# An RWKV-7, convolution and mLSTM block on one core: modulation rows as TensorE products spread through the recurrent chains, a later projection moved into the last chain, and the first dense products by halves

## The chip, the cores and the metric

The kernel runs on one core of one Trainium2 chip. Its five engines have queues of their own: TensorE (PE, with its weight loads PEld), VectorE (DVE), ScalarE (ACT), GpSimd (POOL) and SyncE (SP), which issues the DMAs. An engine takes its instructions in the order of the program and waits on semaphores for the others. The metric is the device time of one execution in microseconds (us).

## The reference

One block is computed in fp32 for 512 tokens of width 1024, with 256 context tokens that only feed the two recurrences. Six modulation vectors come from `silu(c) @ w_ada + b_ada`: shift and scale ahead of the mixers, a gate on their sum, shift and scale ahead of the MLP, and a gate on it.

```python
mod_x = jnp.split((jax.nn.silu(c) @ w_ada[l] + b_ada[l])[:, None, :], N_MOD, axis=-1)
mod_c = jnp.split(jax.nn.silu(c_ctx) @ w_ada[l] + b_ada[l], N_MOD, axis=-1)
h = _rmsnorm(x, g_norm1[l]) * (1.0 + mod_x[1]) + mod_x[0]
hc = _rmsnorm(ctx, g_norm1[l]) * (1.0 + mod_c[1]) + mod_c[0]
u_rw, u_cv, u_ml, u_gate = jnp.split(h @ w_in[l], [OFF_CV, OFF_ML, OFF_GATE], axis=-1)
...
yb = _conv_branch(u_cv, cv_dw[l], cv_db[l], cv_lnw[l], cv_lnb[l], rows)   # silu(layernorm(conv31(a * sigmoid(g))))
x = x + mod_x[2] * _merge(u_gate, ya, yb, yc, p_a[l], p_b[l], p_c[l], w_out[l])
h = _rmsnorm(x, g_norm2[l]) * (1.0 + mod_x[4]) + mod_x[3]
x = x + mod_x[5] * _mlp(h, w_mlp1[l], w_mlp2[l])
```

`ya` is the RWKV-7 mixer (8 heads of 64, a recurrence over the tokens in both directions), `yc` the mLSTM mixer (chunks of 64), and `_merge` is `(sigmoid(ga) * ya@pa + sigmoid(gb) * yb@pb + sigmoid(gc) * yc@pc) @ w_out`.

## The kernel before

Activations lie transposed: a tile holds 128 features by 512 tokens. A dense product is split into high and low parts of both operands: `whalf` (L147) loads half a weight block (`raw`, 128 x 512), ACT makes its high part `whi` (L152) and POOL the low part `wlo` (L153), and PE adds `hi*hh`, `hi*hl` and `lo*hh` for each of eight k-tiles, 24 products of 128 x 512 for a block of 128 columns.

The stages, in program order:
- **Front** (L164 to L231). `norm` scales the rows of x and transposes them on PE (`pl`, L202). For each quarter q of the first two modulation vectors eight products `pr` (L215) with a stationary operand of two columns (c and c_ctx) make a row of 512; four small transposes `pm` (L220) turn it into columns, and `modulate` makes `hh` and `hl` for two k-tiles. All four quarters, then the context norm, stand ahead of the first dense product (L262).
- **Convolution gates and taps** (L273 to L300): two dense blocks make a gated tile `z` (L281), for i = 0 and 1, and 62 DVE operations the depthwise taps; the other two tiles follow in the mLSTM stage, with their taps, from stored `z`. The four results go to DRAM as `yb`.
- **RWKV features**, then **mLSTM** with its dense blocks. `rw.ctx(0)` and `rw.lat(0)` make the first RWKV pair's gram products `pg` (L973) and invert small triangular matrices on DVE.
- **Four chains** (`weave`, L1142). Chain j walks the 12 chunks of head pair j in both directions. A step is a batch of small fp32 products `ch` (L1100, L1106, L1115), with an ACT or DVE operation between batches. Each chain has 36 rounds. Between the batches `weave` puts steps of the next pair's gram and inversion (`PACE` per round), of the tail of the pair before (its group norm), and a number of dense products from one generator: `DENSE[j]` per chain, evenly over the rounds, and `EXTRA[j]` after them. That generator yields the gate products `dg` (L512), then the projections `dp` of the convolution and mLSTM outputs (L591). `paced` keeps a woven instruction behind the batch that it follows.
- **Chain 3** also weaves `conv_norm` (L533, the layer norm and silu of the convolution) and `modulations` (L611): DVE sums `sc[k] * wad` (L608) over 128 x 512 tiles of `w_ada`, eight for each of six quarters, a product with ones closing each. The remaining `dp`, the tail of chain 3 and the remaining sums follow as a drain.
- **Merge and MLP** (`merge`, L1229): the RWKV output's projection `pd` (L682), `w_out` (`pt`, L1268), the second norm, MLP1 (`pd`, L1337), in which the last two quarters of modulation sums (`last_modulation`) stand with one product `pmr` (L644) each, and MLP2 (`pt`).

In PSUM, direction 0 of the gram writes pool PS (tag g), direction 1 pool PSC (tag g).

## Time and profile before

| | |
|---|---|
| time, median of 3 runs | 1372.29 us (1367.92 to 1378.71) |
| the profiled execution | 1377.12 us, its span 1375.3 us |
| PE busy | 1252.9 us (91%) |
| PE weight loads | 969.6 us (71%) |
| DVE busy | 849.2 us (62%) |
| ACT, POOL busy | 511.8 us (37%), 585.7 us (43%) |
| DMA | 187.85 MB, mean 137 GB/s |

Busy shares are means over the span. A row of the chain of waits names what the last work to end was released by, followed back in time. The clock is the TensorE clock that was granted, as a share of the full one; a stretch's mean between 0.5 and 1 is a mixture of two levels. Two PE records belong to one fp32 product.

### The profile page before, as it was taken

The page shows a single profiled execution, that of the slowest core. Times are in us where ns is not written, and L with a number is a line of the kernel's source. Part 1 is how long each engine was busy: PE and PEld are TensorE (multiplying, and loading weights), DVE is VectorE, ACT ScalarE, POOL GpSimd, SP SyncE. Part 2 cuts the span into 40 slices and gives each one's busy share as a digit, 9 for nine tenths or more (in the row PEclk, how much of TensorE's full clock was granted, in tenths as well). Part 3 has the DMA queues.
Part 4 walks back from the last instruction along what each step waited for, and adds up shares of the span by engine and source line. Part 5 has one row for each costly group of instructions (what it writes and reads, how often), then busy time and mean ns, then how long its engine had stood idle before and what let it go on. Part 6 is the DMA issues. An engine that isn't in the chain of part 4 may idle for free.

```text
span 1375.3 us, 21700 instructions
## 1 busy us (share of the span) xinstructions
PE 1252.9 (91%) x8004; PEld 969.6 (71%) x8004; DVE 849.2 (62%) x1509; ACT 511.8 (37%) x1048; POOL 585.7 (43%) x547
## 2 busy tenths in 40 slices
PE   6999989786999886999899988889999999999997
PEld 1587877565888775667566665667888878888886
DVE  2599588889266993797977857678366534300202
ACT  4434556632222231243342444422354444322322
POOL 0443334426755441332433435533456544444442
PEclk9999999898999997999998998999999999999999
DMA  9221588732633314323431244787434433433422
GB/s 375 65 69 58 134 270 255 246 104 62 186 99 97 111 64 120 110 93 101 143 110 49 85 145 136 259 263 249 131 112 156 142 100 95 153 104 96 131 95 89
DMA packets 101457, 187.85 MB, mean 137 GB/s; under 512 B 10708, under 2 KB 29396, under 8 KB 100328
## 3 DMA queue, kind: packets, MB, share of 16 engines
q1 hardware_dynamic: 101352, 186.47, 42.9%
q8 instruction: 63, 1.03, 0.3%
q14 instruction: 42, 0.34, 0.1%
HBM read 148.64 MB, written 29.40 MB: 129 GB/s over the span
## 4 chain that ended last, share of the span: by engine, by line
PE 45%; DVE 14%; DMA 5%; issue 3%; ACT 1%; POOL 1%; SPq 0%; DVEq 0%; POOLq 0%; ACTq 0%
PE pt L1268 16%; PE pd L1337 13%; PE dg L512 5%; DMA wad<-wada 4%; DVE N L1019 3%; DVE tmp L1017 2%; PE pg L973 2%; PE ch L1100 1%; PE pd L682 1%; DVE N L1012 1%; PE ch L1106 1%; DVE accm L608 1%; PE dl L262 1%; PE pbk L998 1%; PE ch L1115 1%
## 5 line engine op out<-in xcount | busy, mean ns | idle before, releaser
L153 POOL TENSOR_TENSOR wlo<-raw,whi 128x512 fp32r<-128x512 f32 x296 | 435.5, 1477 | 555.5 <-ACT whi L152 488.9
L152 ACT CAST whi<-raw 128x512 fp32r<-128x512 f32 x296 | 182.0, 618 | 318.7 <-PE pt L1268 118.8
L262 PE MATMUL dl<-hh,wlo 128*128 128x512 f32 (+1 forms) x368 | 149.7, 407 | 10.8 <-POOL wlo L153 10.8
L262 PE MATMUL dl<-hh,whi 128*128 128x512 f32 (+1 forms) x368 | 151.4, 412 | 2.7 <-ACT kT L758 1.9
L262 PE MATMUL dl<-hl,whi 128*128 128x512 f32 (+1 forms) x368 | 148.5, 403 | 0.0
L1337 PE MATMUL pd<-h2l,whi 128*128 128x512 f32 (+1 forms) x272 | 103.3, 381 | 0.7 <-POOL h2l L1320 0.7
L1337 PE MATMUL pd<-h2h,wlo 128*128 128x512 f32 (+1 forms) x272 | 102.7, 379 | 0.0
L1337 PE MATMUL pd<-h2h,whi 128*128 128x512 f32 (+1 forms) x272 | 101.5, 380 | 0.2 <-ACT h2h L1317 0.2
L1363 DVE TENSOR_TENSOR x<-pt,modb 128x512 f32<-128x512 f32 x8 | 5.5, 690 | 154.7 <-PE pt L1268 154.7
L1268 PE MATMUL pt<-whi,h1h 128*128 128x512 f32 x256 | 99.6, 389 | 0.0
L1268 PE MATMUL pt<-whi,h1l 128*128 128x512 f32 x256 | 99.6, 389 | 0.0
L1268 PE MATMUL pt<-wlo,h1h 128*128 128x512 f32 x256 | 99.1, 389 | 0.0
L262 PEld LDWEIGHTS dl<-hh,wlo 128*128 128x128 f32 (+1 forms) x368 | 70.7, 192 | 26.0 <-POOL wlo L153 11.2
L262 PEld LDWEIGHTS dl<-hh,whi 128*128 128x128 f32 (+1 forms) x368 | 71.2, 193 | 18.6 <-ACT kT L758 2.1
L262 PEld LDWEIGHTS dl<-hl,whi 128*128 128x128 f32 (+1 forms) x368 | 70.8, 192 | 15.2 <-issue 1.5
L608 DVE SCALAR_TENSOR_TENSOR accm<-wad,sc,accm 128x512 f32<-128x512 f32 x56 | 59.1, 1056 | 35.2 <-DMA wad<-wada 34.6
L1113 POOL TENSOR_TENSOR sps<-SV,PL 64x128 f32<-64x128 f32 x88 | 40.0, 454 | 85.1 <-DVE SV L1116 81.9
L1341 DVE TENSOR_TENSOR relu<-relu 128x512 f32<-128x512 f32 x32 | 38.9, 1218 | 55.8 <-ACT relu L1340 55.7
L512 PE MATMUL dg<-hl,whi 128*128 128x512 f32 x144 | 66.5, 462 | 0.0
L512 PE MATMUL dg<-hh,whi 128*128 128x512 f32 x144 | 65.7, 456 | 0.0
L512 PE MATMUL dg<-hh,wlo 128*128 128x512 f32 x144 | 65.6, 456 | 0.0
L1019 DVE TENSOR_TENSOR N<-N,tmp 128x30 f32<-128x30 f32 (+14 forms) x120 | 58.1, 484 | 3.0
(389 smaller groups left out, 2792.3 us busy)
## 6 DMA issues: line engine op xcount, KB each, us to landing
raw<-wblk SPq DMA_DIRECT2D x296, 256.0 KB, 2.9
wad<-wada SPq DMA_DIRECT2D x64, 256.0 KB, 4.0
wada<-wada SPq DMA_DIRECT2D x8, 1024.0 KB, 13.4
BK<-kb SPq DMA_DIRECT2D x16, 384.0 KB, 5.2
sp_bk<-BK SPq DMA_DIRECT2D x8, 768.0 KB, 5.2
BK<-sp_bk SPq DMA_DIRECT2D x8, 768.0 KB, 4.1
sp_g<-gt SPq DMA_DIRECT2D x24, 256.0 KB, 2.0
sp_al<-al SPq DMA_DIRECT2D x8, 640.0 KB, 4.6
```

Of the source, the lines that this page charges most:

```text
L152: A.copy(hi[:, :], raw[:, :])
L153: G.tensor_tensor(lo[:, :], raw[:, :], hi[:, :], ALU.subtract)
L262: PE.matmul(ps_[0:M, :], lhsT=w[:, ko:ko + M], rhs=x[seg][:, k, :], start=(n == 0), stop=(n == 3 * KT - 1))
L512: yield lambda w=w, x=x, k=k, ko=ko, n=n: PE.matmul(ps[:, :], lhsT=w[:, ko:ko + P], rhs=x[:, k, :], start=(n == 0), stop=(n == 3 * KT - 1))
L608: V.scalar_tensor_tensor(o, t[:, :], sc[:, k, 0:1], o, ALU.mult, ALU.add)
L973: PE.matmul(ps[hf, i, :, :], lhsT=BK[dd, c, x, :], rhs=al[:, c] if lat else AL[d][dd, 8 + c:9 + c, :], start=True, stop=True)
L1017: V.tensor_tensor(tv, N[:, s + 1:32, s:s + 1].to_broadcast([P, n, s]), N[:, s:s + 1, 0:s].to_broadcast([P, n, s]), ALU.mult)
L1019: V.tensor_tensor(N[:, s + 1:32, 0:s], N[:, s + 1:32, 0:s], tv, ALU.add)
L1113: last["Pool"] = G.tensor_tensor(sps[hf], SV[d][hf, c, :, :], PL[hf, c, :].unsqueeze(2).to_broadcast([64, 2, CH]), ALU.mult)
L1268: PE.matmul(pss[i][:, :], lhsT=x[:, k, ts_], rhs=w[:, :], start=(k == 0 and n == 0), stop=(k == nk - 1 and n == 2))
L1337: PE.matmul(ps[:, ts_], lhsT=w[:, ko:ko + P], rhs=x[:, k, ts_], start=(k == 0 and n == 0), stop=(k == 7 and n == 2))
L1341: V.tensor_tensor(t[:, :], t[:, :], t[:, :], ALU.mult)
```

## The change

- **Front.** A product of the modulation now has a stationary operand of 32 columns (`scz`, c and c_ctx followed by columns of the next k and zeros) and writes the PSUM rows from 32 * (k mod 4): four consecutive products use four groups of columns of the array. A product with `sel` adds the four partial rows and turns them. All eight `wada` tiles have buffers; the context rows are loaded behind the fifth of them, three weight halves behind the sixth. The first three dense blocks (two gates and one value) are computed by halves: k-tiles 0 to 3 behind quarter 1, k-tiles 4 to 7 behind quarter 3. The context norm stands ahead of quarter 2.
- **Convolution norm.** `conv_norm` moves from chain 3 to behind the second pair of taps; its result goes to DRAM as `yb`. Its tiles share space with the first RWKV pair's.
- **Modulations.** The 64 DVE sums (48 in chain 3 and its drain, 16 in MLP1) become 64 products on PE, one yielded after six gate products, loaded into two `wad` buffers (the load of block n + 2 is issued behind block n). Their rows are closed with `sel`; two vectors go through DRAM and are broadcast on loading. MLP1 has none left.
- **Chains.** `DENSE` becomes 120, 120, 120, 270, so that nearly all `dp` stand in chain 3; `ld` has three buffers. Direction 1 of the gram writes the bank with tag m of pool PS.

PE in the front: the modulation products of the last quarters (`pr`), the closing ones (`pm`), the transposes of context rows (`pl` from `ct`) and the first dense products (`dl`). Before:

```order
L202 MATMUL pl<-cst,xt_180 128x128
L215 MATMUL pr<-wada,sc 2x512 x8
L220 MATMUL pm<-cst,row 128x2 x4
...
L202 MATMUL pl<-cst,xt_180 128x128
L220 MATMUL pm<-cst,row 128x2 x4
L202 MATMUL pl<-cst,ct_198 128x128
L202 MATMUL pl<-cst,ct_200 128x128
L202 MATMUL pl<-cst,ct_198 128x128
...
L202 MATMUL pl<-cst,ct_198 128x128
L202 MATMUL pl<-cst,ct_200 128x128
L262 MATMUL dl<-hh_164,whi 128x512
L262 MATMUL dl<-hl_166,whi 128x512
```
After:

```order
L234 MATMUL pl<-cst,xt_189 128x128
L174 MATMUL pr<-wada,scz 32x512 x8
L189 MATMUL dl<-hh_170,whi 128x512
L189 MATMUL dl<-hl_172,whi 128x512
L189 MATMUL dl<-hh_170,whi 128x512
L189 MATMUL dl<-hl_172,whi 128x512
L234 MATMUL pl<-cst,ct_201 128x128 x2
L254 MATMUL pm<-sel,row 128x2 x4
L189 MATMUL dl<-hh_170,wlo 128x512
...
L189 MATMUL dl<-hh_170,wlo 128x512
L234 MATMUL pl<-cst,ct_203 128x128 x2
L174 MATMUL pr<-wada,scz 32x512 x8
L189 MATMUL dl<-hh_170,whi 128x512
```
All 32 `pr` and the 16 context transposes stood ahead of the first `dl`; now the first `dl` stand behind the third quarter's `pr` and among the transposes, and the fourth quarter's eight `pr` follow 36 of them.

PE in the first steps of chain 0: batches of the chain (`ch`), gate products (`dg`) and, after, one modulation product (`pq`). Before:

```order
L1100 MATMUL ch_4813<-SV_4797,AL_3240 64x64
L1100 MATMUL ch_4813<-SV_4797,AL_3243 64x64
L1100 MATMUL ch_4814<-SV_4798,AL_3241 64x64
L1100 MATMUL ch_4814<-SV_4798,AL_3244 64x64
L512 MATMUL dg<-hh_164,whi 128x512
L512 MATMUL dg<-hl_166,whi 128x512
L1106 MATMUL ch_4813<-xc_4845,LT_3238 64x64 x2
L1106 MATMUL ch_4814<-xc_4849,LT_3238 64x64 x2
L512 MATMUL dg<-hh_164,wlo 128x512
L512 MATMUL dg<-hh_164,whi 128x512
L512 MATMUL dg<-hl_166,whi 128x512
```
After:

```order
L1135 MATMUL ch_4893<-UV_4874,BKt_3329 64x64
L1135 MATMUL ch_4893<-UV_4874,BKt_3330 64x64
L1135 MATMUL ch_4894<-UV_4875,BKt_3329 64x64
L1135 MATMUL ch_4894<-UV_4875,BKt_3330 64x64
L174 MATMUL pq<-wad,scz 32x512
L623 MATMUL dg<-hh_170,whi 128x512
L623 MATMUL dg<-hl_172,whi 128x512
L623 MATMUL dg<-hh_170,wlo 128x512
L1120 MATMUL ch_5007<-SV_4877,AL_3320 64x64
L1120 MATMUL ch_5007<-SV_4877,AL_3323 64x64
```
A round has three gate products in both; the modulation product is one more, beside a batch or between gate products.

PE at the end of chain 3: the outputs of the chain (`py`), its tail (`pm`, `pv`, `pm`), projections of the two other mixers (`dp`) and of RWKV (`pd`). Before (the tail with its neighbours):

```order
L591 MATMUL dp<-yh,whi 128x512
L1193 MATMUL pm<-y,cst 128x512
L591 MATMUL dp<-yl,whi 128x512
...
L591 MATMUL dp<-yh,whi 128x512
L1201 MATMUL pv<-cst,ysq 128x2 x4
L591 MATMUL dp<-yl,whi 128x512
...
L591 MATMUL dp<-yh,wlo 128x512
L1210 MATMUL pm<-cst,rb 128x128 x4
L591 MATMUL dp<-yh,whi 128x512
```
After (the last of `dp`, then the tail):

```order
L663 MATMUL dp<-yh,whi 128x512
L663 MATMUL dp<-yl,whi 128x512
L663 MATMUL dp<-yh,wlo 128x512
...
L1101 MATMUL py<-AL_4870,SV_4878 64x64
L1102 MATMUL py<-LR_4871,UU 64x64
L1210 MATMUL pm<-y,cst 128x512
L1218 MATMUL pv<-cst,ysq 128x2 x4
L1227 MATMUL pm<-cst,rb 128x128 x4
L703 MATMUL pd<-yh,whi 128x512
```
The tail's products stood 22 to 39 `dp` products apart; now they follow one another and the 18 last `dp`, and `pd` stands behind them. Counted over PE's order: gate products in chains 0 to 3 before 110, 104, 120, 98, after 114, 101, 135, 82; modulation products 16, 19, 21, 8; `dp` in chain 3 31 before and 174 after, behind it 161 and 18.

The diff, cut:

```diff
+    def partial(ps, k, w):
+
+
+        g = slice(32 * (k % 4), 32 * (k % 4) + 32)
+        PE.matmul(ps[g, :], lhsT=scz[:, 2 * k:2 * k + 32], rhs=w, start=(k < 4), stop=(k >= 4))
...
+    def first_products(half, wts, pss=None):
+
+        pss = pss or [PSD.tile([P, NT], F32, tag="d", name="dl", bufs=ND) for _ in FIRST]
+        for ps, (hi, lo) in zip(pss, wts):
+            for k in range(4):
+                ko, kt = k * P, half * 4 + k
+                for n, (w, x) in enumerate(((hi, hh), (hi, hl), (lo, hh))):
+                    PE.matmul(ps[:, :], lhsT=w[:, ko:ko + P], rhs=x[0][:, kt, :],
+                              start=(kt == 0 and n == 0), stop=(kt == KT - 1 and n == 2))
...
-        t = S0.tile([P, 4, 512], F32, tag="wada", name="wada", bufs=6)
+        t = S0.tile([P, 4, 512], F32, tag="wada", name="wada", bufs=8)
         SY.dma_start(t[:, :, :], wada[q].rearrange("p (k m) -> p k m", k=4))
         wa.append(t)
-    for i in range(2):
-        t = S0.tile([P, D], F32, name=f"ct{i}")
-        SY.dma_start(t[:, :], cin[i])
-        xt.append(t)
+        if q == 4:
+            for i in range(2):
+                t = S0.tile([P, D], F32, name=f"ct{i}")
+                SY.dma_start(t[:, :], cin[i])
+                xt.append(t)
+        if q == 5:
+            first = [whalf(b, 0) for b in FIRST]
...
         for k in range(KT):
-            PE.matmul(pr[:, :], lhsT=sc[:, k, :], rhs=wa[q * 2 + k // 4][:, k % 4, :], start=(k == 0), stop=(k == KT - 1))
-        row = S0.tile([2, NT], F32, tag="row", name="row", bufs=2)
+            partial(pr, k, wa[q * 2 + k // 4][:, k % 4, :])
+        row = S0.tile([P, NT], F32, tag="row", name="row", bufs=2)
         A.copy(row[:, :], pr[:, :])
...
         for i in range(4):
-            PE.transpose(pt[:, i, :], row[:, i * P:(i + 1) * P], ident[0:2, 0:2])
+            PE.matmul(pt[:, i, :], lhsT=row[:, i * P:(i + 1) * P], rhs=sel[:, :], start=True, stop=True)
         ks = slice(2 * q, 2 * q + 2)
         V.tensor_tensor(modc[:, ks, :], pt[:, 0:2, :], C("b_ada", 2 * q, 2).unsqueeze(2).to_broadcast([P, 2, 2]), ALU.add)
...
-    norm(xt[4:6], NT)
+        if q == 1:
+            head = first_products(0, first)
+    head = first_products(1, [whalf(b, 1) for b in FIRST], head)
     for kt in range(KT):
         modulate(1, kt)
...
     taps(tiles)
-    for i, z, y in tiles:
-        SY.dma_start(sp["yb", i][:, :], y)
+    conv_norm([y for _, _, y in tiles])
...
+    def modulations():
+
+        def load(n):
+            q, k = n // KT, n % KT
+            w = WG.tile([P, NT], F32, tag="wad", name="wad", bufs=2)
+            SY.dma_start(w[:, :], wada[8 + q * 2 + k // 4][:, k % 4 * 512:k % 4 * 512 + 512])
+            return w
+
+        ws = [load(0), load(1)]
+        for q in range(8):
+            ps = rw.PSC.tile([P, NT], F32, tag="pq", name="pq")
+            for k in range(KT):
+                def block(k=k):
+                    partial(ps, k, ws.pop(0)[:, :])
+                    if q * KT + k + 2 < 8 * KT:
+                        ws.append(load(q * KT + k + 2))
+                yield block
+            row = WG.tile([P, NT], F32, tag="gt", name="row", bufs=2)
+            A.copy(row[:, :], ps[:, :])
+            pc = rw.PSC.tile([P, NT], F32, tag="pq", name="pc")
+            if 2 <= q < 6:
+                for i in range(4):
+                    PE.matmul(pc[:, i:i + 1], lhsT=row[:, i * P:(i + 1) * P], rhs=sel[:, 0:1], start=True, stop=True)
+                cs = slice(q % 2 * 4, q % 2 * 4 + 4)
+                if q < 4:
+                    V.tensor_tensor(b2[:, cs], pc[:, 0:4], C("b_ada", 24 + q % 2 * 4, 4), ALU.add)
+                else:
+                    V.tensor_tensor(s2[:, cs], pc[:, 0:4], C("b_ada", 32 + q % 2 * 4, 4), ALU.add)
+                    V.scalar_tensor_tensor(s2[:, cs], s2[:, cs], 1.0, C("g2", q % 2 * 4, 4), ALU.add, ALU.mult)
+            else:
+                m, x = q // 6, slice(q % 2 * 512, q % 2 * 512 + 512)
+                PE.matmul(pc[0:1, :], lhsT=sel[:, 0:1], rhs=row[:, :], start=True, stop=True)
+                br = WG.tile([P, NT], F32, tag="gt", name="br", bufs=2)
+                SY.dma_start(br[0:1, :], rowp[m:m + 1, x])
+                V.tensor_tensor(br[0:1, :], pc[0:1, :], br[0:1, :], ALU.add)
+                SY.dma_start(sp["m", 2 + 3 * m][:, x], br[0:1, :])
...
                     n += 1
+                if k % 2:
+                    f = next(mods, None)
+                    if f:
+                        yield f
...
-    mods = modulations()
-    norm = conv_norm()
-    rw.weave(3, dense_, norm, mods)
+    acc["mod2b"] = acc["pool"].tile([P, D], F32, name="mod2b")
+    SY.dma_start(acc["mod2b"][:, :], sp["m", 2][:, :].partition_broadcast(P))
+    rw.weave(3, dense_)
...
-DENSE = (100, 100, 100, 110)
+DENSE = (120, 120, 120, 270)
 EXTRA = (20, 20, 20, 20)
...
+                ps = self.PS.tile([P, 4, w, CH], F32, tag="gm"[d], name="pg")
 
```

## Rows read from the trace of the kernel before

**Rows 1.** The page: busy time of each engine, then the chain that ended last.
```profile
PE 1252.9 (91%) x8004; PEld 969.6 (71%) x8004; DVE 849.2 (62%) x1509; ACT 511.8 (37%) x1048; POOL 585.7 (43%) x547
...
PE pt L1268 16%; PE pd L1337 13%; PE dg L512 5%; DMA wad<-wada 4%; DVE N L1019 3%; DVE tmp L1017 2%; PE pg L973 2%; PE ch L1100 1%; PE pd L682 1%; DVE N L1012 1%; PE ch L1106 1%; DVE accm L608 1%; PE dl L262 1%; PE pbk L998 1%; PE ch L1115 1%
```

**Rows 2.** Windows: span, busy of PE, PEld, DVE, ACT, POOL, clock, DMA share, GB/s.
```profile
0.00:20.00 20.00, 6.59 (x15) 1.43 (x16) 6.21 (x36) 6.09 (x10) 0.21 (x4) 1.00 0.92 356
...
20.00:40.00 20.00, 20.00 (x67) 5.75 (x66) 9.25 (x26) 9.60 (x19) 4.38 (x4) 1.00 0.82 320
...
72.00:140.00 68.00, 63.17 (x350) 54.65 (x349) 65.64 (x84) 28.14 (x45) 26.22 (x16) 0.97 0.20 64
...
280.00:342.00 62.00, 45.20 (x218) 36.51 (x216) 61.58 (x89) 19.93 (x32) 29.92 (x10) 0.88 0.23 71
...
350.00:450.00 100.00, 97.93 (x710) 83.72 (x709) 55.13 (x168) 26.11 (x49) 55.93 (x63) 1.00 0.41 124
...
538.00:794.00 256.00, 232.35 (x2506) 162.93 (x2506) 198.31 (x402) 90.74 (x270) 90.59 (x129) 0.91 0.34 102
...
794.00:884.00 90.00, 77.99 (x739) 53.55 (x738) 58.32 (x101) 40.78 (x107) 44.24 (x44) 0.91 0.57 179
...
884.00:938.00 54.00, 48.57 (x227) 37.73 (x227) 41.83 (x64) 15.44 (x28) 19.22 (x13) 0.94 0.77 242
```

**Rows 3.** The chain of waits in order of time: start us, us, what held it.
```profile
805.47 6.56 DMA wad<-wada
...
940.25 4.74 DMA wad<-wada
...
1065.92 0.95 PE pmr L644 x2
```

**Rows 4.** Waits, 806 to 906: engine, what it waited for, us, times, longest.
```profile
DVE accm L608 <- DMA wad<-wada: 17.5, 16, 2.5
```

**Rows 5.** Timeline of PE in the front: start us, us, instruction.
```profile
31.32 7.03 PE L215 MATMUL pr<-wada,sc 128*2 128x512 f32 x16
...
53.40 0.52 PE L262 MATMUL dl<-hh,whi 128*128 128x512 f32 x1
...
71.47 0.39 PE L262 MATMUL dl<-hh,whi 128*128 128x512 f32 x1
```

**Rows 6.** Timeline of PE in the first gram.
```profile
408.31 1.09 PE L973 MATMUL pg<-AL,BK 64*64 64x128 f32 x16
```

**Rows 7.** The gated tile `z`: ns min/median/max, first and last start.
```profile
L281 DVE SCALAR_TENSOR_TENSOR z<-tg,dl x2: 681/686/690, 66.3 to 80.7; 128x512 f32<-128x512 f32 x2
```

**Rows 8.** Groups by line, 794 to 884: busy us, mean ns, idle before.
```profile
L550 DVE TENSOR_TENSOR macc<-macc,mean 128x512 f32<-128x512 f32 x4 | 2.7, 737 | 0.0
```

**Rows 9.** Timeline of PE at the end of chain 1.
```profile
698.54 0.39 PE L512 MATMUL dg<-hh,whi 128*128 128x512 f32 x1
...
698.77 0.40 PE L512 MATMUL dg<-hl,whi 128*128 128x512 f32 x1
...
699.10 0.46 PE L1106 MATMUL ch<-xc,LT 64*64 64x64 f32 x8
```

**Rows 10.** Tiles `ch` and `pd`: first and last start of one kind each.
```profile
L1106 PE MATMUL ch<-xc,LT x384: 216/218/367, 544.2 to 883.8; 64*64 64x64 f32 x192
...
L682 PE MATMUL pd<-yh,wlo x32: 387/389/628, 938.9 to 964.4; 128*128 128x512 f32 x32
```

**Rows 11.** The sums of `wad` on DVE, and its loads on the page.
```profile
L608 DVE SCALAR_TENSOR_TENSOR accm<-wad,sc,accm 128x512 f32<-128x512 f32 x56 | 59.1, 1056 | 35.2 <-DMA wad<-wada 34.6
...
wad<-wada SPq DMA_DIRECT2D x64, 256.0 KB, 4.0
```

**Rows 12.** Timeline of all engines in the drain: the tail of chain 3.
```profile
899.61 0.68 DVE L1194 SCALAR_TENSOR_TENSOR y<-pm,y 128x512 f32<-128x512 f32 x1
...
917.28 1.05 PE L1210 MATMUL pm<-cst,rb 128*128 128x128 f32 x8
...
932.23 0.62 ACT L160 CAST yh<-y 128x512 fp32r<-128x512 f32 x1 [3.49 <-POOL y L1221]
```

198 lines of the change are left out of this document (75 added, 123 removed).

## The prediction

> **What bounds the kernel now.** I read the engines' busy shares and the chain of waits first [rows 1]: TensorE (PE) is busy 91% of the span and leads the chain, VectorE (DVE) follows with 62%, and a wait for `wad`, the modulation weights read in the last RWKV chain, holds 4% of the span by itself. These shares are averages over very unlike stages, so the table of stretches comes next [rows 2]. In it the reader is to see four kinds of stage. Up to 53.4 us the modulation rows are made and nothing dense has begun. From 280 to 342 the depthwise taps fill DVE (61.58 of 62 us), and from 350 to 450 PE is full (97.93 of 100). From 538 to 794 the first three chains run: PE is busy 232.35 of 256 us at a mean granted clock of 0.91, so 23.7 us are idle; and since the two clock levels are full and half, 0.09 x 2 = 18% of the stretch, 46 us, ran at half, which makes up to 23 us of its busy time slow work. From 794 to 938 chain 3 and its drain leave 17.4 us idle (12.0 and 5.4), at DMA shares of 0.57 and 0.77. The chain of waits says what holds these last two stretches [rows 3]: 12 pieces of 3.4 to 6.6 us, the first at 805.47 and the last at 940.25, are loads of `wad`, and 17.5 us of DVE's idle time from 806 to 906 end on them [rows 4].
>
> **1. The front.** The eight products of a row group (two records each) took 7.03 us, or 0.88 us each, and 32 of them are 28.1 us of the 53.4 before the first dense product [rows 5]. They used two columns of the array, always the same ones. The change places four consecutive ones in four column groups. The nearest row is a batch of `pg` [rows 6]: 16 records, 8 products of 128 columns, took 1.09 us, while a product of 128 columns at the price of the row group would cost 0.88 x 128/512 = 0.22 us and eight of them 1.76, so two halves of the array gave 1.6 times the rate. The 32 products then cost between 28.1/1.6 = 17.6 us and, if four groups stream together, 28.1/4 = 7.0 us: a gain of 10 to 21 us of PE time. The Trainium skill (TensorEngine Tiling (Array Packing), Key Properties) says that tiles of the array run their weight loads and products in parallel; the `pg` batch agrees in kind, and by the page's full four times the PE gain would be the 21 us.
>
> PE time is not the end there, because loads are. Ahead of the last `wada` tile the queue has 4 x 0.52 + 8 x 1.05 MB, now also 2 x 0.52 MB of context and 3 x 0.26 MB of weights: 12.7 MB with 0.4 of constants. By 20 us 356 GB/s had moved 7.1 MB, and the next 20 us ran at 320 GB/s [rows 2], so the last tile lands near 20 + 5.6/0.32 = 37 us. Behind it stand eight packed products (2 to 4 us), a copy, four sums, the modulation of two tiles, and the part of the 72 halved products that needs them. The first 36 of these are ready to run from about 30 us in waits of PE. All 72 took 18 us before, from 53.40 to 71.47 [rows 5]; with half of them behind the last tile's chain (9 us behind some 43), I set the last at 53 where it was at 72. DVE's first gated tile, at 66.3 [rows 7], can come at 53. The stage after it has PE at 63 and DVE at 66 of 68 us [rows 2], so both matter, and I take the smaller of 19 and 13 with some of the difference: **-15 us** (bounds -5, where the groups don't overlap and only the reordering helps, and -22).
>
> **2. Convolution norm.** It moves from chain 3 into the stage behind the taps. Its DVE work is 16 operations over 512 columns, each at most the 0.74 us of the subtraction [rows 8], and a short reciprocal root: near 12 us. That stage has DVE full until 342, and PE full behind it; the order puts 89 dense products (20 us at 0.23) between the norm and the first `pg`, so PE has cover. What is not covered is DVE's lateness for the later stretch. Zero if all is under PE, 13 if all of it pushes. **+4 us** (0 to +13).
>
> **3. The modulation products in chains 0 to 2.** Of 64 products of 0.88 us, 56 stand in these chains: 49 us. Seven of the eight quarters' closing products add some 4 us, and the chains hold 16 more gate products, 3.7 us at 0.23. That is 57 us of PE in 256 us that had 23.7 idle. Within a quarter their column groups alternate, but a block stands among dense products, six gate products from the next, so there is no second block to overlap: the gain of part 1 does not come here. Each block switches the array's shape twice; a dense product beside a chain batch starts 0.33 us after the one before it, against 0.23 between dense products (699.10 after 698.77, 698.77 after 698.54) [rows 9], so 56 blocks might pay up to 56 x 2 x 0.1 = 11 us more; a third of the blocks stand beside a chain or `pg` batch that switched anyway, or can overlap its 64-column halves, and I put the two against each other at zero. The Trainium skill (TensorEngine Tiling (Array Packing), Key Properties) has a rule against this change: to change the tiling mode drains the array. By that rule every switch would be paid.
>
> What absorbs the 57 us? The idle 23.7 us, as far as blocks fall where a chain batch waits for ScalarE or DVE, and the up to 23 us lost at half clock, as far as steadier work raises it. Both in full leaves +11, neither +57. The blocks are placed by count, one for six gate products, not by where a wait is, so I take 40% of the 47: **+38 us** (+11 to +57; +68 with every switch paid).
>
> **4. Chain 3 and the drain.** They took 794 to 964.8 = 171 us (the last chain batch at 883.8, the projection of the RWKV output from 938.9 to 964.4 [rows 10]). 48 sums on DVE (1.06 us each) leave these stretches [rows 11], and with them the 17.5 us of waits [rows 4]. Now 174 of the `dp` products stand in the chain (before 31) and 82 gate products (before 98): 127 more, 29.2 us, and 8 blocks, 7 us: 36 us. Of the idle time (12 us) and the half clock (0.09 x 90 = 8 us) I let 60% absorb it, more than in part 3, since DVE's sums leave these steps: 90 + 24 = 114 us. The drain shrinks from 54 us to the 13 `dp` products after the last chain batch (3 us), and the tail of chain 3, which before lay under 161 `dp` products: DVE's first step at 899.61, the last tail product at 917.28, the split at 932.23 [rows 12]. Its bare operations up to the last product are four of a 512-column kind on ScalarE and DVE (0.7 us each, as at 899.61), three sets of products (1 us each, as at 917.28) and eleven short DVE steps (estimated at 0.2): 8 us, with hand-overs 8 to 10, now uncovered on PE; behind them 27 `pd` products (6 us) cover most of the remaining POOL and split steps. With the projection itself (25.5 us, and 0.4 for its last product) this gives 3 + 10 + 26 = 39 us. 114 + 39 = 153 against 171: **-18 us** (-5 to -33). Of DMA, `wad` loads move to the chains before, where the share was 0.34 [rows 2]; the `ld` loads of g come earlier in one stretch of 0.57.
>
> **5. MLP.** Two products of 0.95 us on the chain, one at 1065.92 and its twin behind the next eight blocks, go away [rows 3]: **-2 us**.
>
> **Sum.** -15 + 4 + 38 - 18 - 2 = +7 us. The profiled execution took 1377.1 us, so 1384 by its own time; it lies 4.8 us above the median of three, 1372.3 us (1367.9 to 1378.7). On the median's footing the time is **1379 us**. That is inside 1%, 13.7 us, about what a measurement of this kernel can tell from no change.
>
> **Rivals.**
> - *Absorbed blocks (faster).* The modulation products run in the chains' waits and keep the clock up. For it: 47 us of idle and slow time lie in that stretch, and gate products are already the filler there. Against it: PE is at 91% busy, and the idle time belongs to the steps in which DVE works, while blocks are spread evenly. With +11 in part 3, -20 in part 1 and -25 in part 4: -32, so 1340 us.
> - *Column groups don't overlap.* For it: no row here has 32-column products in four groups. Against: `pg`. Part 1 gives -5, so 1389 us.
> - *Modulation loads stall the chains (slower).* `wad` has two buffers, and each load is queued on SP until PE has finished the block two before; behind it on SP stand raw weights of the gates and the chains' `SV` and `AL` loads. A load took 4.0 us in the median and up to 6.6 [rows 3, 11]. Two blocks are on average 2 x 256/56 = 9 us apart, so it is hidden when evenly spaced; it decides where blocks stand closer than some 6 us, in the dense-rich steps. With a 0.5 us stall per block, 56 x 0.5 = 28: 1407 us.
> - *Nothing absorbed.* +57 in part 3: 1398 us.
> - *Every switch paid.* A change between products of 128, 64 and 32 columns costs its 0.1 us [rows 9] at each of 112 places, also beside batches: +11, so 1390 us. The gap at 699.10 speaks for it; against it, a third of the blocks stand where a batch switches anyway. The Trainium skill's rule on draining (the same page and section) is what would make it so.
> - The second `pg` direction takes the bank that `pbk` and `px` use. A wait there makes the gram steps longer; I price it in the range only.
>
> **How the numbers follow.** Forecast, no change within 1%: 0.37. Absorbed blocks, with the milder mixtures of it and a large front gain: 0.27, faster by over 1%. No overlap in the front 0.10, stalled loads 0.11, nothing absorbed 0.08, every switch paid 0.07: together 0.36, slower by over 1%. The range goes from 1350, which leaves out only the fullest absorption (about 0.1), to 1408, just past the stalled loads (0.1 above). The likeliest case alone is 1366 to 1386.
>
> **What would show it.** Part 1: the row products in 2 to 4 us per quarter or not, and DVE's first gated tile near 53. Part 2: the first `pg` of the gram no later, relative to the taps' end, by more than 4 us. Part 3: the length from the first to the last chain batch of chains 0 to 2 (some 250 us before) near 290, with PE's idle share and clock; a block's own duration 0.88, and waits of PE on `wad`. Part 4: from the last chain batch to the first product of the output projection 36 to 42 us where it was 81. It is wrong if the chains grow by less than 20 us or more than 60, or the front gains under 8.

## The result, and the profile after

| | before | after |
|---|---|---|
| time, median (lowest to highest) | 1375.5 us (1367.9 to 1379.3), 4 runs | 1415.6 us (1410.6 to 1419.6), 4 runs |
| ratio | | 1.030 [1.023, 1.036] |
| span of the profiled execution | 1375.3 us | 1408.8 us |

The change made the kernel 3% slower: 37 us over the forecast and 8 us past the range's upper end. The page's row of PE, and its row of the modulation products in the chains:

```profile
PE 1292.0 (92%) x8148; PEld 975.2 (69%) x8148; DVE 810.8 (58%) x1451; ACT 516.3 (37%) x1056; POOL 561.0 (40%) x547
...
L174 PE MATMUL pq<-wad,scz 128*32 128x512 f32 x128 | 66.4, 642 | 1.1 <-DMA wad<-wada 0.5
```

Against [rows 1] PE has 39 us more work and DVE 38 us less: the sums changed engine, and PE is the engine without room. The next row's wait is a rival's answer: in all four chains these products waited 0.5 us for `wad`, not 28. In chains 0 to 2 alone PE is busy 293.4 us against 232.4 [rows 2], 61 us more, and idle 17.2 against about 20, counted from the first batch.

Stretches of after, with the columns of [rows 2]: the taps' start, chains 0 to 2, chain 3, the tail behind the last chain batch, the output projection, and from there to the end of MLP1:

```profile
72.00:140.00 68.00, 60.79 (x332) 51.95 (x331) 62.54 (x83) 30.67 (x48) 21.90 (x15) 0.95 0.20 61
...
547.70:858.30 310.60, 293.41 (x2868) 177.01 (x2868) 209.54 (x413) 100.14 (x290) 89.90 (x126) 0.93 0.44 130
858.30:956.10 97.80, 97.32 (x670) 65.84 (x669) 40.70 (x71) 40.34 (x104) 43.73 (x48) 1.00 0.60 192
956.10:969.70 13.60, 8.29 (x63) 6.31 (x59) 5.48 (x18) 2.67 (x7) 0.00 (x0) 0.84 0.00 1
969.70:998.70 29.00, 27.27 (x113) 21.40 (x113) 19.44 (x23) 10.53 (x18) 14.59 (x10) 0.96 0.67 227
998.70:1226.70 228.00, 226.32 (x1026) 184.77 (x1025) 95.62 (x118) 97.25 (x183) 111.31 (x87) 0.99 0.31 101
```

Some of its tiles (ns minimum, median, maximum; first and last start), answering to [rows 7, 10]:

```profile
L316 DVE SCALAR_TENSOR_TENSOR z<-tg,dl x2: 675/682/690, 60.7 to 71.5; 128x512 f32<-128x512 f32 x2
L1126 PE MATMUL ch<-xc,LT x384: 216/218/366, 550.7 to 956.1; 64*64 64x64 f32 x192
L703 PE MATMUL pd<-yh,wlo x32: 388/394/628, 970.8 to 998.7; 128*128 128x512 f32 x32
L1351 PE MATMUL pd<-h2h,wlo x272: 278/399/415, 1043.4 to 1226.7; 128*128 128x512 f32 x120, 128*128 128x256 f32 x16
```

Read as a ledger of the two profiled executions: the first batch `xc` of the chains stands 6.5 us later (550.7 against 544.2), the batches run 65.8 us longer (405.4 against 339.6), from the last batch to the first `pd` it is 41 us less (13.6 against 54.6), the projection takes 2.9 more, what lies between it and MLP1 3.0 less, MLP1 2.4 more (186.3 from its first product to its last, against 183.9). The sum is the 33.5 us between the spans. The first entry is the least sure: `e3_noblocks`, `e4_group4`, `e5_full` and `e6_pad` below have nearly the same instructions up to the chains, and their first batch `xc` stands at 556.8, 560.0, 554.6 and 553.3.

### The profile page after: what moved, and what is told of

It reads as the page before. It is cut to its first block, busy times and chain, and to the rows that moved or that the text cites. A ratio compares the mean times of both kernels' runs of the same rounds, so it can differ in the third digit from the quotient of the medians.

```text
span 1408.8 us, 21891 instructions
## 1 busy us (share of the span) xinstructions
PE 1292.0 (92%) x8148; PEld 975.2 (69%) x8148; DVE 810.8 (58%) x1451; ACT 516.3 (37%) x1056; POOL 561.0 (40%) x547
## 5 line engine op out<-in xcount | busy, mean ns | idle before, releaser
L160 POOL TENSOR_TENSOR wlo<-raw,whi 128x512 fp32r<-128x512 f32 x296 | 411.7, 1396 | 511.0 <-ACT whi L159 428.1
L295 PE MATMUL dl<-hh,whi 128*128 128x512 f32 (+1 forms) x344 | 143.4, 417 | 3.7 <-DVE lf L718 2.2
L295 PE MATMUL dl<-hh,wlo 128*128 128x512 f32 (+1 forms) x344 | 139.8, 407 | 0.0
L295 PE MATMUL dl<-hl,whi 128*128 128x512 f32 (+1 forms) x344 | 139.5, 405 | 0.0
L1355 DVE TENSOR_TENSOR relu<-relu 128x512 f32<-128x512 f32 x32 | 43.6, 1366 | 84.7 <-ACT relu L1354 84.7
L295 PEld LDWEIGHTS dl<-hh,whi 128*128 128x128 f32 (+1 forms) x344 | 67.0, 195 | 19.2 <-issue 4.4
L295 PEld LDWEIGHTS dl<-hh,wlo 128*128 128x128 f32 (+1 forms) x344 | 66.7, 194 | 14.3 <-issue 0.4
L174 PE MATMUL pq<-wad,scz 128*32 128x512 f32 x128 | 66.4, 642 | 1.1 <-DMA wad<-wada 0.5
L996 DVE TENSOR_TENSOR LT<-pg,cst 64x256 f32<-64x256 f32 x48 | 20.1, 420 | 77.5 <-PE pg L993 75.6
L623 PE MATMUL dg<-hl,whi 128*128 128x512 f32 x144 | 60.9, 423 | 0.0
```

Source lines behind the costliest of these rows:

```text
L160: G.tensor_tensor(lo[:, :], raw[:, :], hi[:, :], ALU.subtract)
L174: PE.matmul(ps[g, :], lhsT=scz[:, 2 * k:2 * k + 32], rhs=w, start=(k < 4), stop=(k >= 4))
L295: PE.matmul(ps_[0:M, :], lhsT=w[:, ko:ko + M], rhs=x[seg][:, k, :], start=(n == 0), stop=(n == 3 * KT - 1))
L623: yield lambda w=w, x=x, k=k, ko=ko, n=n: PE.matmul(ps[:, :], lhsT=w[:, ko:ko + P], rhs=x[:, k, :], start=(n == 0), stop=(n == 3 * KT - 1))
L996: V.tensor_tensor(LT[dd, h * 12 + c4 * 4:h * 12 + c4 * 4 + 4, :], ps[dd, :, w - 1, :], m_[dd, :, w - 1, :], ALU.mult)
L1355: V.tensor_tensor(t[:, :], t[:, :], t[:, :], ALU.mult)
```

## The experiments

Ratios are to the kernel before, timed on the same chip beside it. The mean granted clock of one run differs from the next, and over 63 runs of the kernel before the time fell by 9.1 us for each 0.01 of clock (correlation -0.78). So differences under 10 us are taken from medians, and a single profile shows where, not how much.

### Without the blocks, and four in a row

`e3_noblocks` is the changed kernel without its 64 blocks, their loads and closings; an empty step stands in the place of each.

```diff
                 def block(k=k):
-                    partial(ps, k, ws.pop(0)[:, :])
-                    if q * KT + k + 2 < 8 * KT:
-                        ws.append(load(q * KT + k + 2))
+                    pass
                 yield block
```

> The changed kernel without its 64 modulation products in the chains, their loads and their closing products (the four later modulation vectors are then only their biases); every other instruction keeps its place in the count. Theory: a product costs the PE its 0.88 us and nothing hides it, so 64 of them and the closing ones are 56 to 62 us: about 1355 us, ratio to the kernel before 0.985. Rival 1: a third or more of them lies in idle time of PE or is given back by the clock: 20 to 40 us, 1375 to 1395 us. Rival 2: each costs more than its 0.88 us by the switch of the array's shape or by its load: 68 us or more, below 1348 us.

Measured: 1360.9 us, ratio 0.989 [0.986, 0.993]. Against after (1.030) that is 55 us, about 45 to 65 by the two intervals, for 64 blocks: 0.86 us each, closings included. That is near the theory's 56 to 62, so little was absorbed. Its runs have a mean clock of 0.943 against 0.949 in after, so by the slope above the price at an equal clock would be some 5 us higher. Its first three chains, in the columns of [rows 2]:

```profile
556.80:805.00 248.20, 226.45 (x2643) 163.88 (x2642) 203.05 (x402) 93.83 (x278) 89.38 (x124) 0.94 0.33 102
```

PE is idle for 21.8 of 248 us; after has 17.2 idle of 311. So the 56 blocks in these chains filled some 5 us of waits. Against that, at the clock 0.93 after has 0.14 x 311 = 43 us at half clock, this kernel 0.12 x 248 = 30: the blocks took no slow time away.

`e4_group4` collects the blocks: one step behind each 24 gate products issues four products in the four column groups, with four `wad` buffers (and smaller constants, to make room for these).

```diff
-            w = WG.tile([P, NT], F32, tag="wad", name="wad", bufs=2)
+            w = WG.tile([P, NT], F32, tag="wad", name="wad", bufs=4)
...
-                if k % 2:
-                    f = next(mods, None)
-                    if f:
-                        yield f
+                if k == 7:
+                    fs = [f for f in (next(mods, None) for _ in range(4)) if f]
+                    if fs:
+                        yield lambda fs=fs: [f() for f in fs]
+                elif k % 2 and g < NGA + 16:
+                    yield lambda: None
```

> The changed kernel with its modulation products issued four in a row behind every 24 gate products (four buffers instead of two, small vectors kept in place of copies to make room), so that four column groups stand side by side. Theory: four together took 1.0 us in the front instead of 3.5 alone, so 16 groups save 16 x 2.5 = 40 us: about 1376 us, ratio to the kernel before 1.00. Rival: the blocks' cost lies in switches of shape and waits on loads, of which a group has a quarter as many, too, but four loads now land together: if loads hold the groups, PE waits on wad appear and less than 20 us are saved, above 1395 us.

Measured: 1378.1 us, ratio 1.000 [0.996, 1.004]: 37 us less than after by the medians, 40 by the ratios, with about 10 either way. Its timeline of PE (start, us, instruction), four products as eight records between two gate products:

```profile
574.05 0.50 PE L623 MATMUL dg<-hh,wlo 128*128 128x512 f32 x1
574.48 1.06 PE L174 MATMUL pq<-wad,scz 128*32 128x512 f32 x8
575.48 0.50 PE L623 MATMUL dg<-hh,whi 128*128 128x512 f32 x1
```

Four products take 1.0 us from start to start. In after one takes as long:

```profile
700.24 0.39 PE L623 MATMUL dg<-hh,wlo 128*128 128x512 f32 x1
700.56 1.05 PE L174 MATMUL pq<-wad,scz 128*32 128x512 f32 x2
701.54 0.46 PE L1135 MATMUL ch<-UV,BKt 128*64 128x64 f32 x8
```

The 64 single blocks are 64 x 0.98 = 63 us of PE, sixteen groups 16. The 47 us between them came out as 37 to 40, so PE's time in the chains is nearly the kernel's time.

### The price of a change of the array's shape

`e5_full` gives the blocks of the chains a stationary operand of 128 columns (only the first is used), so that beside dense products the shape doesn't change. The closings read the same rows.

```diff
-                    partial(ps, k, ws.pop(0)[:, :])
+                    PE.matmul(ps[:, :], lhsT=scz[:, 2 * k:2 * k + P], rhs=ws.pop(0)[:, :], start=(k == 0), stop=(k == KT - 1))
```

> The changed kernel with the modulation products of the chains over a stationary operand of all 128 columns (c and c_ctx, columns of the next k and zeros) into one accumulation, so that no narrow tile stands between the dense products; the front keeps its four groups. Theory: a lone product pays for its 512 columns at 0.88 us and nothing for its width: 1415 us, ratio to the kernel before 1.03. Rival: the switch to a 32-column tile and back costs 0.1 us or more each: 64 x 0.2 = 13 us less, about 1402 us, ratio 1.02. A third case: a narrow block overlaps the chain's 64-column halves beside it, which a wide one can't: slower than 1415 by up to 8 us.

Measured: 1409.8 us, ratio 1.028 [1.021, 1.034], against 1.030 [1.023, 1.036] for after. Its timeline of PE between a gate product and a batch, to set beside the rows of after just above:

```profile
708.12 0.39 PE L623 MATMUL dg<-hh,wlo 128*128 128x512 f32 x1
708.35 1.02 PE L589 MATMUL pq<-wad,scz 128*128 128x512 f32 x2
709.30 0.46 PE L1126 MATMUL ch<-xc,LT 64*64 64x64 f32 x8
```

From the gate product to the block it is 0.23 us here and 0.32 in after; from the block to the batch, where the shape changes in both, 0.95 and 0.98. Between gate products more of it shows; first after, then `e5_full`:

```profile
567.70 0.50 PE L623 MATMUL dg<-hh,wlo 128*128 128x512 f32 x1
568.14 1.04 PE L174 MATMUL pq<-wad,scz 128*32 128x512 f32 x2
569.11 0.50 PE L623 MATMUL dg<-hh,whi 128*128 128x512 f32 x1
569.45 0.40 PE L623 MATMUL dg<-hl,whi 128*128 128x512 f32 x1
```

```profile
570.65 0.50 PE L623 MATMUL dg<-hh,wlo 128*128 128x512 f32 x1
570.99 1.02 PE L589 MATMUL pq<-wad,scz 128*128 128x512 f32 x2
571.45 0.79 PE L623 MATMUL dg<-hh,whi 128*128 128x512 f32 x1
572.08 0.40 PE L623 MATMUL dg<-hl,whi 128*128 128x512 f32 x1
```

From the first product to the last it is 1.75 us with the narrow block and 1.43 with the wide one (six places of this form in each trace: 1.63 to 1.75 and 1.32 to 1.43). So the narrow shape costs a block 0.3 us of PE between gate products and 0.1 ahead of a batch, which for 64 blocks is an estimate of 6 to 20 us. What its removal is worth in the time isn't resolved: 6 us by the medians, 3 by the ratios, some 12 either way. So the 11 us of the rival that every switch is paid are neither shown nor excluded. In its chains 0 to 2 the freed PE time came back in part as idle time, 24 us where after has 17.2. The Trainium skill (TensorEngine Tiling (Array Packing), Key Properties) says that a change of tiling mode drains the array; the 0.1 to 0.3 us may be that drain, and no run here separates it from other causes.

### The front alone

`e1_front` is the kernel before with the new front only; `e9_frontpad` is the same with 96 bytes of constants per partition ahead of the pools (below).

```diff
         for k in range(KT):
-            PE.matmul(pr[:, :], lhsT=sc[:, k, :], rhs=wa[q * 2 + k // 4][:, k % 4, :], start=(k == 0), stop=(k == KT - 1))
+            partial(pr, k, wa[q * 2 + k // 4][:, k % 4, :])
...
+        if q == 1:
+            head = first_products(0, first)
+    head = first_products(1, [whalf(b, 1) for b in FIRST], head)
```

> The kernel before with the new front alone (four column groups, first dense blocks by halves, context norm ahead of quarter 2, moved loads). Theory: in the changed kernel the fourth dense block began 11.3 us earlier, but VectorE's first gated tile only 5.6 us earlier, and by the second pair of taps 5.7 us were left, since VectorE, not PE, bounds the stage behind; alone the front is then worth 4 to 7 us: ratio 0.995 to 0.997, about 1369 us. Rival: the gain of 11 us was eaten only by what stands behind in the changed kernel, and alone it is worth 10 to 12 us: ratio 0.992, about 1364 us.

> The kernel before with the new front alone, now with 96 bytes more of constants, so that the weights stand at 224 mod 256 bytes as before. Theory: the front is worth 6 to 8 us where chain 0 starts (8 us earlier in the run without the padding), and it measured zero there because the operands' place took 6 to 8 us back in MLP1 and the projections: ratio 0.994 to 0.996, about 1368 us. Rival: VectorE's taps and the chains swallow the front's gain and the padding alone gives back less: 0.998 or more.

Measured: `e1_front` 1378.4 us, ratio 1.000 [0.997, 1.004]; `e9_frontpad` 1379.5 us, ratio 1.000 [0.997, 1.004]. Both theories had a gain of 4 us or more, and both missed. The front is worth nothing in the time, though their profiles have the first chain batch at 536.2 and 537.5 where [rows 10] has 544.2:

```profile
L1141 PE MATMUL ch<-xc,LT x384: 216/218/367, 536.2 to 879.2; 64*64 64x64 f32 x192
L1143 PE MATMUL ch<-xc,LT x384: 216/218/367, 537.5 to 873.0; 64*64 64x64 f32 x192
```

Where the gain goes shows first in `e1_front`, in its chain 1; the second row is chain 1 of the kernel before:

```profile
611.00:707.00 96.00, 85.46 (x903) 60.50 (x902) 74.64 (x142) 31.41 (x92) 30.68 (x42) 0.82 0.32 97
```

```profile
620.60:705.70 85.10, 76.94 (x904) 54.53 (x903) 71.01 (x142) 31.26 (x92) 30.65 (x42) 0.92 0.36 108
```

The same instructions take 11 us more at a granted clock of 0.82. By the end of the output projection this execution has 4 us of its lead left, and MLP1, whose operands the new front moved (below), takes 188.6 us where it took 183.9. The profiled execution of `e9_frontpad`, with MLP1 at 183.9 again, does keep its lead, with a span of 1364.6 us; it is the fastest of its ten runs, at a mean clock of 0.955. The ten have 0.944, the runs of the kernel before beside them 0.951, and 0.007 of clock is 6 us by the slope above. So at an equal clock its ratio of 1.000 would be a gain of some 6 us, about the lead. Whether the new front lowers the clock, or the chip did in these runs, stays open. In `e1_front` the clocks lie closer (0.949 against 0.951, 2 us), and the 4.7 us of MLP1 make up most of the rest.

### The convolution norm alone

`e2_norm` is the kernel before with the norm behind the second taps.

```diff
     taps(tiles)
-    for i, z, y in tiles:
-        SY.dma_start(sp["yb", i][:, :], y)
+    conv_norm([y for _, _, y in tiles])
...
-    norm = conv_norm()
+    norm = iter(())
```

> The kernel before with the convolution norm alone moved behind the second pair of taps; chain 3 then only loads its result. Theory: the norm costs the mLSTM stage 10 to 12 us (its VectorE work, and PE at half clock around it), and since chain 3 was held by the loads of the modulation weights, chain 3 gives back only 2 to 5: ratio 1.004 to 1.007, about 1382 us. Rival: the stage behind the taps has cover, the cost there is 4 us and chain 3 gives back as much: ratio 1.000, 1375 us. The profile decides by the time from the end of the taps to the first batch of chain 0 (186 us before, 201 in the changed kernel).

Measured: 1375.0 us, ratio 1.001 [0.997, 1.004]: the rival's ratio, though not by its way, which had 4 us in either place. In its profile the chains begin 13 us later, about the norm's DVE time, and 11 of these are back by the end of the projection. The waits of the sums for `wad` are little changed, 30.6 us where [rows 11] has 34.6, while the sums themselves take 51.5 where they took 59.1:

```profile
L603 DVE SCALAR_TENSOR_TENSOR accm<-wad,sc,accm 128x512 f32<-128x512 f32 x56 | 51.5, 920 | 31.4 <-DMA wad<-wada 30.6
```

So chain 3 and what follows it gave back about what the norm costs the early stage, though their loads still held the sums; moved, the norm is worth nothing.

### The place of the operands

MLP1 had grown though work left it. `e6_pad` is the changed kernel and `e7_before_pad` the kernel before, each with one unused tile of 96 bytes per partition ahead of everything, which moves the later tiles; not an instruction of MLP1 changes.

```diff
     par = K.tile([P, NPARAM], F32, name="par")
+    shift = K.tile([P, 24], F32, name="shift")
+    nc.vector.memset(shift[:, :], 0.0)
```

> The changed kernel with 96 bytes of unused constants more per partition, nothing else. The new front's constants moved every tile of the weight pools by 160 bytes; in MLP1 the moving operand h2h stands at 224 mod 256 bytes, the weights stood there, too, before, and at 128 mod 256 now. In the kernels with the new front the products of MLP1 follow one another at 0.2329 us, in those without it at 0.2266. Theory: it is the place of the two operands relative to each other; with 96 bytes more the weights are at 224 again, MLP1 and the projections return to 0.2266, and 5 to 7 us go: about 1409 us. Rival: the spacing belongs to something else in the front's kernels (the order, the loads): no change, 0.2329 and 1415 us.

> The kernel before with the same 96 bytes of unused constants, nothing else: its weights go to 64 mod 256 bytes, h2h stays at 224. By the theory of the operands' place MLP1 goes from 0.2266 to 0.2329 us a product and the kernel is 5 to 7 us slower: ratio 1.004 to 1.005. By the rival (something else in the front's kernels) nothing changes: ratio 1.000, 0.2266.

Measured: `e6_pad` 1411.1 us, ratio 1.027 [1.021, 1.032]; `e7_before_pad` 1382.6 us, ratio 1.006 [1.003, 1.009]. The timelines of PE in MLP1 (after, `e6_pad`, the kernel before, `e7_before_pad`):

```profile
1129.91 0.39 PE L1351 MATMUL pd<-h2l,whi 128*128 128x512 f32 x1
1130.14 0.40 PE L1351 MATMUL pd<-h2h,wlo 128*128 128x512 f32 x1
...
1130.85 0.40 PE L1351 MATMUL pd<-h2h,wlo 128*128 128x512 f32 x1
```

```profile
1129.92 0.39 PE L1353 MATMUL pd<-h2h,wlo 128*128 128x512 f32 x1
...
1130.60 0.39 PE L1353 MATMUL pd<-h2h,wlo 128*128 128x512 f32 x1
```

```profile
1100.03 0.39 PE L1337 MATMUL pd<-h2h,wlo 128*128 128x512 f32 x1
...
1100.71 0.39 PE L1337 MATMUL pd<-h2h,wlo 128*128 128x512 f32 x1
```

```profile
1099.55 0.39 PE L1339 MATMUL pd<-h2h,wlo 128*128 128x512 f32 x1
...
1100.25 0.39 PE L1339 MATMUL pd<-h2h,wlo 128*128 128x512 f32 x1
```

Three products take 0.71 us in after, 0.68 with the tile; 0.68 in the kernel before, 0.70 with the tile. Within either pair nothing but the place of the operands in a partition differs for these products. By the layout of the tiles, which no trace shows, the activations `h2h` lie at 224 (modulo 256 bytes) in all kernels here; the weights `whi` at 224 in the kernel before and in `e6_pad`, at 128 in after and `e1_front`, at 96 in `e4_group4`, at 64 in `e7_before_pad`. The two fast ones are those with equal remainders. MLP1 from first to last product shows it whole: without sums in it 180.2 us in `e6_pad` and 184.9 in `e3_noblocks`, with them 183.9 before and 188.6 in `e1_front`. That is 4.7 us in either pair; the sums that left it gave 3.7. `e9_frontpad`, which is `e1_front` with the 96 bytes, is a third pair: 183.9. So it is shown that 96 bytes switch the spacing, in three kernels and both ways; that the equal remainder decides is argued from the layouts. In the time only `e7_before_pad` is clear of its reference: `e6_pad` against after is 4 us, within the intervals.

### The blocks elsewhere, and the two unpriced edits

`e8_early` is `e6_pad` with all modulation products taken out of the chains: in the mLSTM stage, about half of them while DVE has the taps, sixteen steps of four products each, one 1 MB load for each step. Empty steps stand in the chains where blocks stood.

```diff
+            for h in range(2):
+                def block(h=h):
+                    w = ws.pop(0)
+                    for k in range(4):
+                        partial(ps, 4 * h + k, w[:, k, :])
...
+    some(8)
     st[0] = front(0)
+    some(4)
     st[1] = front(1)
+    some(5)
```

> The changed kernel with its later modulations moved out of the chains into the mLSTM stage, in fours (one load of 1 MB for four products side by side), with 96 bytes of padding as above; the chains keep the count of their dense products. Theory: 16 groups of 1.0 us and the closing products are 20 us of PE in a stage that VectorE's taps fill while PE idles 17 of 62 us; so nearly all of the 55 us that the products cost in the chains goes, and 6 more by the padding: 1355 to 1362 us, ratio 0.985 to 0.99. Rival: the 16.8 MB of loads, 60 to 80 us at the stage's rates, hold up the dense weights on the same queue, or delay the gram that waits for the space: 10 to 20 us come back, 1370 to 1378 us.

Measured: 1361.3 us, ratio 0.993 [0.989, 0.996]: by the ratios 47 us less than `e6_pad`, and inside the theory's 1355 to 1362.

Two edits of the change had stood in the prediction as a sum (the projections in chain 3) and as a range only (the bank). `e10_dense` is `e8_early` with the projections spread as before, `e11_bank` is `e8_early` with direction 1 of the gram in the other pool's bank, as before; `e12_best` has both.

```diff
-DENSE = (120, 120, 120, 270)
+DENSE = (100, 100, 100, 110)
...
-                if k % 2 and g < NGA + 16:
-                    yield lambda: None
```

```diff
-                ps = self.PS.tile([P, 4, w, CH], F32, tag="gm"[d], name="pg")
+                ps = self.PG[d % len(self.PG)].tile([P, 4, w, CH], F32, tag="g", name="pg")
```

> The kernel with the modulations in the mLSTM stage (e8), with the kernel before's counts of woven products (100, 100, 100, 110, no places held for modulations), so that 161 or so of the projections of the other two mixers fall behind the last chain again. Theory: chain 3 has little idle PE time left to hide them in, so weaving them (the changed table) gave 5 to 15 us by covering the tail's ScalarE and VectorE steps less and the chain's waits more: 1366 to 1376 us, ratio 0.994 to 1.001. Rival 1: the weave is worth the 18 us that I took for chain 3 and the drain: 1379 us. Rival 2: PE is the bound in both places, and it is worth nothing: 1361 us.

> The kernel with the modulations in the mLSTM stage (e8), with the gram's second direction back in a PSUM bank of its own (free again, since no modulation product needs it in the chains). Theory: the shared bank costs little, since the gram's batches wait for VectorE anyway: 1359 to 1362 us. Rival: pg of the second direction waits for the products that share its bank (pbk, px): 8 us or more in the gram of the chains, about 1353 us, ratio 0.986 or less.

> Both together: modulations in fours in the mLSTM stage, the kernel before's counts of woven products, the second gram direction in its own bank, 96 bytes of padding. Theory: neither the count nor the bank was worth more than 5 us, so 1355 to 1361 us, ratio 0.985 to 0.990, clear of the kernel before. Rival: e10 and e11 were lucky draws of the clock (4 runs each), and together they are no better than e8: 1361 to 1364 us, ratio 0.990 to 0.993.

Measured: `e10_dense` 1357.3 us, 0.989 [0.984, 0.995]; `e11_bank` 1360.8 us, 0.990 [0.985, 0.995]; `e12_best` 1343.4 us, 0.979 [0.975, 0.982]. Each alone is within its interval of `e8_early`; together they give 18 us, more than their theory or their rival had, and `e12_best` is 29 us faster than the kernel before. But its six runs have a mean clock of 0.962, where `e8_early` has 0.949, `e10_dense` 0.948, `e11_bank` 0.953, and the kernel before beside them 0.951 to 0.953. By the slope above, 12 of the 18 us and 9 of the 29 go with that clock, and at an equal clock `e12_best` and `e10_dense` would be 20 and 17 us ahead of the kernel before, nearly alike. Whether the two edits together raise the clock, or these runs had it by chance, stays open. Chain 3, what follows it and the output projection, in `e8_early` (woven) and in `e12_best` (spread, with the first three chains ahead):

```profile
828.00:926.00 98.00, 94.72 (x841) 69.73 (x841) 50.20 (x73) 43.73 (x111) 44.68 (x48) 0.97 0.56 175
926.00:940.70 14.70, 9.38 (x66) 7.26 (x63) 6.08 (x19) 2.67 (x7) 0.00 (x0) 0.79 0.00 1
940.70:969.00 28.30, 26.16 (x113) 20.97 (x112) 19.29 (x24) 11.09 (x19) 15.06 (x10) 0.99 0.71 236
```

```profile
553.60:800.50 246.90, 225.97 (x2504) 158.24 (x2503) 199.11 (x400) 90.38 (x270) 89.16 (x124) 0.94 0.33 101
800.50:868.10 67.60, 64.84 (x718) 44.59 (x717) 27.35 (x53) 36.65 (x102) 31.84 (x38) 1.00 0.58 183
868.10:911.00 42.90, 41.93 (x214) 33.81 (x210) 22.45 (x41) 13.20 (x24) 17.38 (x13) 1.00 0.57 186
911.00:932.50 21.50, 21.50 (x96) 17.82 (x95) 18.20 (x21) 7.49 (x13) 7.74 (x6) 1.00 0.49 169
```

Woven, the three stretches are 141 us; spread, 132. The other pair says the same: 142 in `e11_bank`, 132 in `e10_dense`. For `e10_dense` the theory had a loss of 5 to 15 us from spreading; the sign was wrong. The tail's waits (5.3 us idle, no transfer under way) and a projection of 28.3 us come with the weave. Spread, the `dp` products cover the tail, PE is idle for 3.7 us in 132, and the projection takes 21.5. It is the drain of [rows 2], there 54 us at a DMA share of 0.77, here 42.9 at 0.57, with DVE's sums and their loads gone from it.

## Why the prediction was wrong, point by point

**What bounds the kernel** was read rightly and taken too lightly: with PE at 91%, the products moved onto it were paid nearly in full. Of the marks set for the changed kernel, the front's products at 1.0 us for four and the absence of waits for `wad` came as forecast; the first gated tile stands at 60.7 and not near 53, the first three chains take 311 us and not 290.

**Part 3 failed, and is with part 1 the larger part of the error.** The counts held. Chains 0 to 2 took 311 us from their first batch where they took 252, so +58 and not +38. What failed is the absorption, 40% of 47 us of idle and slow time, 19 us: PE got 61 us more work there (57 in the prediction) and its idle time fell by 2.5 us, while the time at half clock stayed at some 45 us (0.18 x 252 before, 0.14 x 311 after). Of the 64 blocks the prediction left some 39 us in the sum (60 for the products and closings of both parts, less the 19 of part 3 and the 2 that fall to the blocks in part 4). `e3_noblocks` measured 55, with 10 either way. The rival "nothing absorbed" was nearly the right mechanism. Its price for the whole kernel, 1398, fell short because the front was still counted in it. The switches, which the prediction set against overlaps at zero, do take PE time (0.1 to 0.3 us for a block), so a part of the +58 may be theirs; `e5_full` doesn't resolve how much.

The reason it named against absorption fits the profiles: chain waits are the waits of one step, the blocks come by count. The hope that steadier work raises the clock is not borne out (0.94 without the blocks, 0.93 with them, over a longer stretch).

**Part 1 failed.** The groups do stream together, at nearly the upper bound. Timeline of PE in after's front:

```profile
16.27 1.09 PE L174 MATMUL pr<-wada,scz 128*32 128x512 f32 x8
...
28.02 1.07 PE L174 MATMUL pr<-wada,scz 128*32 128x512 f32 x8 [2.10 <-DMA wada<-wada]
...
46.24 1.92 PE L174 MATMUL pr<-wada,scz 128*32 128x512 f32 x16
...
60.71 0.50 PE L295 MATMUL dl<-hh,whi 128*128 128x512 f32 x1
```

Four products take 1.0 us where one took 0.88 [rows 5]. The Trainium skill (TensorEngine Tiling (Array Packing), Theoretical Speedup) gives up to four times for 32 columns, and this trace agrees: 4 x 0.88 against 1.0 us is 3.5 times. But the last quarter's products, which I set behind the last `wada` tile near 37 us, stand at 46.24: in PE's order they follow 36 dense products and the context transposes, and these ran in a stretch of waits and slow clock. The longest wait, 2.6 us, is for DVE's part of the context norm, which the change had moved ahead of them:

```profile
30.30:46.20 15.90, 13.22 (x48) 10.45 (x48) 7.79 (x13) 4.79 (x9) 7.66 (x6) 0.69 0.46 177
```

At 0.69 some 62% of that stretch is at the half level. The loads came as forecast: the DMA share is 0.92 from 27 to 37 us and 0.17 from there to 46.2. So the fourth dense block begins at 60.71 where it was at about 72, 11 us and not 19; DVE's gated tiles come 5.6 and 9.2 us earlier, the chains 7 to 8 in both kernels with the front alone, and the median not at all. -15 came out as 0 (within 5 us); the terms that failed are PE's order and clock in the front, which cost 8 of the 19 us, and the step from a lead at the chains to the end.

**Part 2 held** in its range: some +13 at the chains in the profile, as its bound had it, and 0 in the time, since chain 3 and the projection gave it back, a relief that no term of the sum had.

**Part 4 held in kind, and gave more than forecast.** The stretch from the start of chain 3 to the end of the projection went from 171 us to 140 in the profiled pair (97.8 us of chain, 13.6 and 29.0), so -30, where -18 was forecast. Before, the last transposes of the inversions (7.6 us of DVE) still stood behind 794, after they end ahead of chain 3, so a few us may belong to part 3 instead. Taken together, chains, drain and projection were to give +20 and gave +28. The 13.6 us tail is the 11 to 13 that the sum had. What the prediction didn't weigh is the alternative: with DVE relieved, the old spread takes some 10 us less than the weave in the profiles (`e10_dense`, `e12_best`), though `e10_dense` alone doesn't show it in the median.

**Part 5 had the wrong sign for a reason not in it.** The sums that left MLP1 gave 3.7 us (forecast 2); the constants of the new front moved the weight tiles, and that cost 4.7. The rest of the 2.4 is within what profiles differ by.

**Rivals.** Stalled loads: false, 0.5 us. No overlap in the front: false. Every switch paid: PE pays them, the time is not resolved. Absorbed blocks: false. Nothing absorbed: nearly true.

Of the 37 us, 3 are the footing: the kernel before ran at 1375.5 beside this one, and the forecast stood on 1372.3. The other 33: 16 from the blocks, 15 from the front, 4 from MLP1 (+2.4 for -2), less 4 for the norm, are 31. Each of these is uncertain by 5 to 10 us, so that they nearly add up proves little. And the 3.0% against the kernel before, as steps between ratios: `e12_best` -2.2%, then the weave and the bank +1.4%, the products in the chains instead of ahead of them +3.4%, the place of the operands +0.3% (the last within the intervals). The first is what the whole change is worth when its products stand ahead of the chains and the old spread and bank are kept; 0.7 of it goes with the higher clock of these runs.

## What to carry to other kernels

Work moved onto the engine that bounds the kernel costs nearly its full duration, unless a wait is named into which it falls; spread by count it filled almost none here (5 of 22 us). If it must go there, put narrow products next to each other where they can share the array (64 single ones cost 55 us, sixteen groups of four some 15 to 18), and in a stage whose bound is another engine. And a lead in an early stage is not a gain until the end shows it: compare medians, since a single profile's clock moves a kernel like this one by 10 us.

## What the runs showed of the hardware that I had not expected

The spacing of dense products depends on where their operands lie: three of them in 0.68 us where, by the layout, weights and activations had the same remainder modulo 256 bytes, in 0.70 to 0.71 otherwise. An unused tile of 96 bytes made one kernel 0.6% slower, and shortened MLP1 of the other from 186.3 to 180.2 us.

A lone product of 32 columns among wider ones took longer than one of 128 in its place: ahead of a batch 0.1 us more, and between dense products 0.3 us more (1.75 against 1.43 us from the product before it to the second behind). Four in different column groups take as long as one (1.0 us).
